# Loading a second layer's weight granules from another engine's queue, one block pair ahead of their split

## The chip, the cores and the metric

One Trainium2 chip, of which the program uses one core. Its engines are named as the profile names them: PE is TensorE's matmuls (PEld its weight loads), DVE is VectorE, ACT is ScalarE, POOL is GpSimd, and SP is SyncE, whose queue issues transfers. The metric is device time in microseconds (us) of one execution, the median of several runs. Less is better.

## The reference, cut to what matters

One inference step of two layers on 4096 prompt rows and 8 sample rows, in float32, width 1024. Layer 0 projects the normalized rows with a 1024 x 3072 matrix, mixes (pooling in four groups, a short convolution, gates), and projects back with a 1024 x 1024 matrix onto the residual. Layer 1 is a windowed attention whose input projection has 2560 columns.

```python
def even_layer(x, ...):          # layer 0
    p = einsum('btd,de->bte', rms_norm(x, g_norm), w_in)
    u, z_a, b_gate, c_gate, v_in, z_b = split(p, EVEN_SPLITS)
    d = pool_mix(u, ...)
    y_a = blockdiag(d, pool_w) * pool_scale * silu(z_a)
    y_b = b_gate * short_conv(c_gate * v_in, ...) * silu(z_b)
    return x + concat(y_a, y_b) @ w_out
# layer 1: q, k, v, z = split(rms_norm(x, g) @ w_in_odd); o = sliding_window_attention(q, k, v)
#          x = x + (o * silu(z)) @ w_out_odd
```

## The kernel before, in words

Every product is made of three passes over a high and a low part of both factors, so each weight is first split: ScalarE writes the high part (a copy to a rounded type), VectorE the difference. `split` (line 80) and `parts` (line 206) do that.

**Layer 0** (lines 176 to 746) runs over six chunks of rows, `L0_CHUNKS`: one of 384, four of 768, one of 640. For each chunk `mixers` goes through 12 pairs of 128-column blocks of the input projection (`pair`, line 444), and `outproj` (line 657) then makes the output projection in two halves of 512 columns. From the second chunk on a pair is a two-by-two product with seven partial products instead of eight, 84 matmuls of 128x384, in an order that is written out in lines 480 to 497: `px`, `py` and `pz` are its three banks of PSUM, and between the products ScalarE copies a bank away (`kept`: first `p1`, then `u2`, then `p5`) before TensorE may add the next product to that bank or VectorE may use it. Each pair first gets its weights by `operands`: four loads on SP's queue, split as they come (tiles `wr`, `wh`, `wl`, three buffers each).

A half of `outproj` is 144 matmuls of 128x512: four quarters `q`, each with one loaded weight tile (`wro`, split to `who` and `wlo`), times six row tiles. Each row tile has a bank (`pso`). When a tile's last quarter is done, VectorE adds the residual (`xr`, loaded by SP in line 668) to it (line 711), SP stores the sum (line 712), and the bank is free for the same row tile of the second half. There are two buffers for `xr`: a third tile's residual is loaded only when the first tile's sum has been stored.

**Layer 1's weights** are prepared during layer 0's chunks 2 to 5: `wq` is a list of 56 granules of 128 x 512. `convert` (line 267), called once a pair and twice in pairs 5 and 11, so 14 times a chunk, does this: it stores the granule of the call before (line 272, SP, 512 KB), loads a new one into a buffer (line 279 or 281, SP, 256 KB), and splits it (ScalarE line 287, VectorE line 288; for the last 16 granules lines 69 and 72). The buffers `cv` have the tag "x", of which there are two, so a load waits for the store of the granule two before it. Layer 1 reads the split granules later.

**Order.** In layer 0 the program text does not fix where an instruction stands in its engine's queue: the framework's scheduler places each as soon as its inputs are expected, and each engine then works through its own queue in that order. The granules of a chunk are therefore not spread over its 12 pairs but stand around the end of the previous chunk's `outproj` and the chunk's first pairs.

Of the kernel before, what the change touches and what calls it, by code (L numbers as in the profile page):

```python
# [9 lines left out]
F32R = mybir.dt.float32r  # L10
U8 = mybir.dt.uint8
AF = mybir.ActivationFunctionType
ALU = mybir.AluOpType
# [4 lines left out]
P = 128  # L18
# [36 lines left out]
def hybrid_kernel(  # L55
# [7 lines left out]
    act, dve, pool, pe, sp = nc.scalar, nc.vector, nc.gpsimd, nc.tensor, nc.sync  # L63

    def f(ap):
        return ap.bitcast(F32)
# [13 lines left out]
    def split(hi, lo, src):  # L80
        acopy(hi, src)
        sub(lo, src, f(hi))
# [15 lines left out]
    gt = cst.tile([P, 2, KT], F32, tag="gt", name="gt")[:, 0]  # L98
# [12 lines left out]
    def granule(key):  # L111

        kind, c, k = key
        if kind == "z":
            e0 = 1536 + c * 256
            return w_in1[:, 2 * k:2 * k + 2, e0:e0 + 256], [2 * k, 2 * k + 1]
        if kind == "in":
            return w_in1[:, k, c:c + 512], [k]
        return w_out1[:, k, c:c + 512], []

    wq = {key: dram.tile([P, 2, 512], F32, tag=f"wq{i}", name=f"wq{i}") for i, key in enumerate(
        z_cols(range(4)) + cols("in", 0) + cols("in", 1024) + cols("in", 512) + cols("out", 0)
        + cols("out", 512))}
# [52 lines left out]
    with ExitStack() as l1:  # L176
# [3 lines left out]
        xp = l1.enter_context(tc.tile_pool(name="xp1", bufs=2))  # L180
# [81 lines left out]


        todo = list(wq)
        converted = []

        def convert(n=1):

            for _ in range(n):
                if converted:  # L270
                    key, t = converted.pop()
                    sp.dma_start(wq[key], f(t))
                if todo:
                    key = todo.pop(0)
                    t = xp.tile([P, 2, 512], F32R, tag="x", name="cv", bufs=2)
                    raw = f(t[:, 1])
                    src, gains = granule(key)
                    if len(gains) > 1:
                        sp.dma_start(raw.rearrange("p (k e) -> p k e", k=2), src)
                    else:  # L280
                        sp.dma_start(raw, src)
                    if not gains:
                        split(t[:, 0], t[:, 1], raw)
                    w = 512 // max(len(gains), 1)
                    for i, kt in enumerate(gains):
                        c = slice(i * w, i * w + w)
                        act.activation(t[:, 0, c], raw[:, c], AF.Copy, scale=gt[:, kt:kt + 1])
                        dve.scalar_tensor_tensor(out=t[:, 1, c], in0=raw[:, c],
                                                 scalar=gt[:, kt:kt + 1], in1=f(t[:, 0, c]),
                                                 op0=ALU.mult, op1=ALU.subtract)  # L290
                    converted.append((key, t))

        def load_out(src):
            raw = wp.tile([P, 2, 512], F32, tag="wr", name="wro", bufs=3)
# [131 lines left out]
        def mixers(ci, X, yh, yl, side=iter(())):  # L426
            t0, n = L0_CHUNKS[ci]
# [5 lines left out]
            w = WX = L + hs  # L433
# [10 lines left out]
            def pair(i, blocks, out11, out12, out22, mid=None):  # L444

                if plain:
                    for e in range(2):
                        wh, wl = block_parts(blocks[e], e == 1)
                        ps = bank("ps")
                        for kt in range(KT):  # L450
                            for k, (u_, v_) in enumerate(((wh, hh), (wh, hl), (wl, hh))):
                                pe.matmul(ps, lhsT=u_[:, kt // 4, kt % 4, :], rhs=v_[:, kt, :],  # L452
                                          start=kt == 0 and k == 0, stop=kt == KT - 1 and k == 2)
                        if e == 0:
                            out11(ps, None)
                            if mid is not None:
                                mid()
                    return ps
                gr = operands(ci, i)
                if ci > 1:  # L460
                    convert(2 if i in (5, 11) else 1)

                def mm(ps, a, b, start=False):


                    gi, at = AT[a]
                    wh, wl = gr[gi]
                    xh, xl, o = B[b]
                    for kt in range(4):
                        for i, (u_, v_) in enumerate(((wh, xh), (wh, xl), (wl, xh))):  # L470
                            pe.matmul(ps, lhsT=u_[:, at, kt, :], rhs=v_[:, o, kt, :],  # L471
                                      start=start and kt == 0 and i == 0, stop=kt == 3 and i == 2,
                                      skip_group_check=True)

                def kept(ps, name):
                    t = tp.tile([P, WX], F32, tag="cp", name=name, bufs=2)[:, :w]
                    acopy(t, ps)
                    return t

                x = bank("px")  # L480
                mm(x, "A11", "B11", start=True)
                p1 = kept(x, "p1")
                y = bank("py")
                mm(y, "A12", "B21", start=True)
                out11(y, p1)
                if mid is not None:
                    mid()
                mm(x, "S2", "T2")
                u2 = kept(x, "u2")
                z = bank("pz")  # L490
                mm(z, "S1", "T1", start=True)
                p5 = kept(z, "p5")
                mm(x, "S3", "T3")
                out22(x, p5)
                mm(z, "S4", "B22")
                out12(z, u2)
                mm(x, "A22", "T4")
                return x

            def plus(out, a, b):  # L500
# [15 lines left out]
            for g in range(4):  # L516
# [76 lines left out]
                for pi in range(NP):  # L593
                    vv, c = vs[pi], cs_[pi]
                    src = c21 if pi == 0 else vv[:, 2:2 + w]
# [5 lines left out]
                    t = tp.tile([P, WX], F32, tag="dl", name="t")  # L601
                    dve.tensor_scalar(out=t[:, :L], in0=vv[:, 0:L], scalar1=cw[:, 0, g:g + 1],
                                      scalar2=None, op0=ALU.mult)
                    for k in (1, 2):
                        dve.scalar_tensor_tensor(out=t[:, :L], in0=vv[:, k:k + L],
                                                 scalar=cw[:, k, g:g + 1], in1=t[:, :L],
                                                 op0=ALU.mult, op1=ALU.add)
# [125 lines left out]
        for ci in range(1, len(L0_CHUNKS)):  # L733
            n = L0_CHUNKS[ci][1]
            last = ci + 1 == len(L0_CHUNKS)
            yh, yl = (yp.tile([P, KT, n + (NS + 40 if last else 0)], F32R, tag=t, name=t)
                      for t in ("yh", "yl"))
            mixers(ci, nxt, yh, yl)
            if not last:
                side = prep(ci + 1)  # L740
                nxt = next(side)
                for _ in side:
                    pass
            if last:
                convert()
            outproj(ci, yh, yl, yh[:, :, n + NS:] if last else None)

    DEBUG = globals().get("DEBUG_L1")
# [11 lines left out]
    xp = ctx.enter_context(tc.tile_pool(name="xp2", bufs=1))  # L760
# [768 lines left out]
```

## Time and profile before

| what | value |
|---|---|
| median of three runs | 3276.95 us (3274.37 to 3279.48) |
| the profiled execution | 3273.23 us |
| its span, first to last instruction | 3271.5 us |
| mean granted TensorE clock | 0.984 of full speed |
| PE busy in the span | 3088.4 us |
| DMA | 541.85 MB, nearly all by SP's queue |

The profile is of one execution; its time is below the lowest of the three runs. A stretch is given in us from the span's start. The granted clock is a share of 2.4 GHz. "Idle before" of an instruction is the time in which its engine had nothing to do, with the instruction or transfer whose end let it go on.

### The profile page before, as it was taken

What the parts mean: (1) busy time and instruction counts of PE and PEld (TensorE: products, weight loads), DVE (VectorE), ACT (ScalarE), POOL (GpSimd) and SP (SyncE); (2) the same over time, 40 slices, a digit from 0 to 9 for tenths busy, and PEclk for the clock granted to TensorE, in tenths of its full rate; (3) what the DMA queues carried; (4) which work ended last, traced back from release to release, by engine and by line L of the source; (5) the groups of instructions that cost most, each with busy time, mean ns of one, the idle gap of its engine ahead of it and who ended that gap; (6) DMA issues with size and microseconds to landing.
All of it is one profiled execution on the core that took longest, in us unless ns stands there. A gap on an engine that the chain in (4) does not pass through costs nothing.

```text
span 3271.5 us, 46047 instructions
## 1 busy us (share of the span) xinstructions
PE 3088.4 (94%) x15926; PEld 2673.6 (82%) x15926; DVE 2148.7 (66%) x4244; ACT 1600.6 (49%) x3701; POOL 870.6 (27%) x1229
## 2 busy tenths in 40 slices
PE   7999999999999999998999999999999999999877
PEld 7888889979979979977778888888878788876665
DVE  5668757767767667831675866758668576685851
ACT  4433434444444444422574655646547466463650
POOL 3244201101111010001332542535325244243420
PEclk9999999999999999999999999999999999999988
DMA  6453375366356357436435546355454553533333
GB/s 186 133 174 127 126 243 172 123 226 206 126 195 229 127 170 262 142 122 222 158 105 187 184 148 216 135 193 184 142 210 142 183 193 136 206 119 123 108 109 134
DMA packets 297922, 541.85 MB, mean 166 GB/s; under 512 B 25272, under 2 KB 159040, under 8 KB 297649
## 3 DMA queue, kind: packets, MB, share of 16 engines
q1 hardware_dynamic: 297689, 538.91, 48.5%
q8 instruction: 126, 2.06, 0.3%
q14 instruction: 107, 0.88, 0.1%
HBM read 462.91 MB, written 78.24 MB: 165 GB/s over the span
## 4 chain that ended last, share of the span: by engine, by line
PE 57%; DVE 16%; DMA 9%; ACT 8%; issue 5%; POOL 5%; SPq 1%; DVEq 0%; POOLq 0%; ACTq 0%
PE px L471 11%; PE pst L838 6%; PE pst L840 6%; PE pst L839 6%; PE pz L471 6%; ACT s L1107 3%; PE ps L452 2%; PE py L471 2%; PE pso L691 2%; PE pso L689 2%; PE pso L693 2%; DMA xr<-x 2%; PE sc L1083 2%; DMA xr<-in_x_prompt_dram 1%; PE psz L927 1%
## 5 line engine op out<-in xcount | busy, mean ns | idle before, releaser
L69 ACT ACTIVATE wh<-wr 128x1024 fp32r<-128x1024 f32 x240 | 227.7, 950 | 231.4 <-PE pz L471 83.4
L211 DVE TENSOR_TENSOR wl<-wr,wh 128x1024 fp32r<-128x1024 f32 x228 | 251.5, 1107 | 104.4 <-ACT wh L69 104.2
L838 PE MATMUL pst<-w,hh 128*128 128x512 f32 x768 | 309.4, 403 | 3.6 <-DVE xr L75 3.5
L840 PE MATMUL pst<-w,hh 128*128 128x512 f32 x768 | 303.5, 395 | 0.0
L839 PE MATMUL pst<-w,hl 128*128 128x512 f32 x768 | 302.7, 394 | 0.0
L1107 ACT ACTIVATE s<-s,st,rq 128x128 f32<-128x128 f32 x512 | 247.2, 484 | 100.1 <-DVE st L1103 99.5
L1127 POOL TENSOR_SCALAR_AFFINE_SELECT qh<-ph 128x512 fp32r<-128x512 f32 x124 | 89.1, 718 | 721.7 <-ACT ph L69 703.7
L471 PE MATMUL px<-th,wh 128*128 128x384 f32 (+1 forms) x720 | 240.4, 334 | 15.0 <-ACT u L69 10.5
L471 PE MATMUL px<-th,wl 128*128 128x384 f32 (+1 forms) x720 | 238.3, 331 | 0.0
L471 PE MATMUL px<-tl,wh 128*128 128x384 f32 (+1 forms) x720 | 238.3, 331 | 0.0
L838 PE MATMUL pst<-w,yh 128*128 128x512 f32 x512 | 209.7, 410 | 8.3 <-DVE xr L75 8.2
L926 PE MATMUL psz<-hh,w 128*128 128x512 f32 x512 | 208.2, 407 | 0.3 <-ACT q L69 0.3
L689 PE MATMUL pso<-who,yh 128*128 128x512 f32 x512 | 201.7, 395 | 6.0 <-DVE xr L75 6.0
L840 PE MATMUL pst<-w,yh 128*128 128x512 f32 x512 | 203.8, 398 | 0.0
L927 PE MATMUL psz<-hl,w 128*128 128x512 f32 x512 | 203.6, 398 | 0.0
L928 PE MATMUL psz<-hh,w 128*128 128x512 f32 x512 | 203.4, 397 | 0.0
L839 PE MATMUL pst<-w,yl 128*128 128x512 f32 x512 | 203.1, 397 | 0.0
L691 PE MATMUL pso<-who,yl 128*128 128x512 f32 x512 | 202.8, 396 | 0.0
L693 PE MATMUL pso<-wlo,yh 128*128 128x512 f32 x512 | 201.6, 394 | 0.0
L838 PEld LDWEIGHTS pst<-w,hh 128*128 128x128 f32 x768 | 145.5, 189 | 31.6 <-DVE xr L75 6.0
L840 PEld LDWEIGHTS pst<-w,hh 128*128 128x128 f32 x768 | 145.1, 189 | 31.6
L839 PEld LDWEIGHTS pst<-w,hl 128*128 128x128 f32 x768 | 145.5, 189 | 25.9
(348 smaller groups left out, 8616.6 us busy)
## 6 DMA issues: line engine op xcount, KB each, us to landing
w<-wq SPq DMA_DIRECT2D x448, 512.0 KB
wr<-in_w_in_even_dram SPq DMA_DIRECT2D x96, 512.0 KB
wr<-wsc SPq DMA_DIRECT2D x96, 512.0 KB
wq<-cv SPq DMA_DIRECT2D x56, 512.0 KB
wro<-in_w_out_even_dram SPq DMA_DIRECT2D x48, 512.0 KB
xr<-in_x_prompt_dram SPq DMA_DIRECT2D x64, 256.0 KB
x<-xr SPq DMA_DIRECT2D x64, 256.0 KB
xt<-x SPq DMA_DIRECT2D x32, 512.0 KB
```

The costliest lines, as they stand in the source:

```text
L69: return act.activation(out, in_, AF.Copy)
L211: (eng or dve).tensor_tensor(out=wl[:, :n], in0=raw, in1=f(wh[:, :n]), op=ALU.subtract)
L471: pe.matmul(ps, lhsT=u_[:, at, kt, :], rhs=v_[:, o, kt, :], start=start and kt == 0 and i == 0, stop=kt == 3 and i == 2, skip_group_check= ...
L689: pe.matmul(acc[i], lhsT=yh[:, kt, ts_], rhs=wh[:, e, :], start=kt == 0, stop=False)
L691: pe.matmul(acc[i], lhsT=yl[:, kt, ts_], rhs=wh[:, e, :], start=False, stop=False)
L693: pe.matmul(acc[i], lhsT=yh[:, kt, ts_], rhs=wl[:, e, :], start=False, stop=kt == KT - 1)
L838: pe.matmul(acc[i], lhsT=xh(kt), rhs=wh, start=kt == 0, stop=False)
L839: pe.matmul(acc[i], lhsT=xl(kt), rhs=wh, start=False, stop=False)
L840: pe.matmul(acc[i], lhsT=xh(kt), rhs=wl, start=False, stop=kt == KT - 1)
L926: pe.matmul(acc[e], lhsT=wh[:, k, es], rhs=xh, start=kt == 0, stop=False)
L927: pe.matmul(acc[e], lhsT=wh[:, k, es], rhs=xl, start=False, stop=False)
L1107: C["exp"] = act.activation(s[:, h, :], s[:, h, :], AF.Exp, bias=nm[:, h:h + 1], scale=r4[:, h:h + 1], accum_out=den[:, h:h + 1])
```

## The change

The three steps of `convert` become three functions. `conv_load` loads a granule, now from ScalarE's queue (`act.dma_start`); `conv_split` splits the granule loaded by the call before; `conv_store` stores it, from SP's queue as before. A pair starts with a split and the next load; in pairs 5 and 11 a store, a split and a load follow in its middle; every pair ends with a store. Buffers, sizes, values and the number of granules stay as they are.

```diff
-        converted = []
-        def convert(n=1):
-            for _ in range(n):
-                if converted:
-                    key, t = converted.pop()
-                    sp.dma_start(wq[key], f(t))
-                if todo:
...
-                    if len(gains) > 1:
-                        sp.dma_start(raw.rearrange("p (k e) -> p k e", k=2), src)
-                    else:
-                        sp.dma_start(raw, src)
...
-                    converted.append((key, t))
+        loaded, parted = [], []
+        def conv_load():
+            if todo:
+                key = todo.pop(0)
+                t = xp.tile([P, 2, 512], F32R, tag="x", name="cv", bufs=2)
+                raw = f(t[:, 1])
+                src, gains = granule(key)
+                act.dma_start(raw.rearrange("p (k e) -> p k e", k=2) if len(gains) > 1 else raw, src)
+                loaded.append((key, t, gains))
+        def conv_split():
+            if loaded:
+                key, t, gains = loaded.pop(0)
...
+                parted.append((key, t))
+        def conv_store():
+            if parted:
+                key, t = parted.pop(0)
+                sp.dma_start(wq[key], f(t))
...
                 gr = operands(ci, i)
                 if ci > 1:
-                    convert(2 if i in (5, 11) else 1)
+                    conv_split()
+                    conv_load()
...
                 if mid is not None:
                     mid()
+                if ci > 1 and i in (5, 11):
+                    conv_store()
+                    conv_split()
+                    conv_load()
                 mm(x, "S2", "T2")
...
                 mm(x, "A22", "T4")
+                if ci > 1:
+                    conv_store()
                 return x
```

What the change does to the queues is shown at three places, all around the end of the first chunk of 768 rows. Lines of the changed kernel have other numbers: its 678 is 668 of before, 722 is 712, 273 and 294 are the load and the store of a granule, 285 the split.

SP's queue, while the first half of `outproj` ends: `xr_3836`, `xr_3840`, `xr_3844`, `xr_3848`, `xr_3852` and `xr_3856` are the residuals of the six row tiles, `x1_3` to `x1_8` the stores of their sums. Before:

```order
L712 DMA x1_3_63<-xr_3836 128x512
L712 DMA x1_4_64<-xr_3840 128x512
L668 DMA xr_3844<-in_x_prompt_dram 128x512
L219 DMA wr_4064<-in_w_in_even_dram 128x8x128
L668 DMA xr_3848<-in_x_prompt_dram 128x512
L246 DMA wr_4070<-wsc0_185 128x1024
L712 DMA x1_5_65<-xr_3844 128x512
L272 DMA wq0_102<-cv_4088 128x1024
L712 DMA x1_6_66<-xr_3848 128x512
L668 DMA xr_3852<-in_x_prompt_dram 128x512
L272 DMA wq1_103<-cv_4241 128x1024
L668 DMA xr_3856<-in_x_prompt_dram 128x512
```

and of the change, after the store of `x1_3`:

```order
L678 DMA xr_3844<-in_x_prompt_dram 128x512
L722 DMA x1_4_64<-xr_3840 128x512
L219 DMA wr_4064<-in_w_in_even_dram 128x8x128
L722 DMA x1_5_65<-xr_3844 128x512
L678 DMA xr_3848<-in_x_prompt_dram 128x512
L294 DMA wq0_102<-cv_4088 128x1024
L678 DMA xr_3852<-in_x_prompt_dram 128x512
L246 DMA wr_4070<-wsc0_185 128x1024
L722 DMA x1_6_66<-xr_3848 128x512
L294 DMA wq1_103<-cv_4240 128x1024
L722 DMA x1_7_67<-xr_3852 128x512
L678 DMA xr_3856<-in_x_prompt_dram 128x512
```

The load of the fourth residual (`xr_3848`) moved from before the third sum's store to behind it, the store of the fourth sum from before to behind the load of the fifth residual, and the load of the sixth from before to behind the store of the fifth sum. The same holds at the ends of the next two chunks; at the fourth, the order of residual loads and stores is the same, with the granules' stores at other places between them.

TensorE's queue in the second half of that `outproj`, whose banks `pso_3860` to `pso_3865` follow those of the first half's six row tiles, at the place where the fifth bank is first used. Before:

```order
L689 MATMUL pso_3863<-who_3910,yh_1662 128x512
L691 MATMUL pso_3863<-who_3910,yl_1663 128x512
L693 MATMUL pso_3863<-wlo_3911,yh_1662 128x512
L689 MATMUL pso_3863<-who_3910,yh_1662 128x512
L689 MATMUL pso_3864<-who_3868,yh_1662 128x512
L691 MATMUL pso_3864<-who_3868,yl_1663 128x512
```

and of the change:

```order
L701 MATMUL pso_3860<-who_3910,yl_1663 128x512
L703 MATMUL pso_3860<-wlo_3911,yh_1662 128x512
L699 MATMUL pso_3861<-who_3910,yh_1662 128x512
L701 MATMUL pso_3861<-who_3910,yl_1663 128x512
L699 MATMUL pso_3864<-who_3868,yh_1662 128x512
L701 MATMUL pso_3864<-who_3868,yl_1663 128x512
```

Counted from the half's first matmul, the fourth bank is first used after 22 matmuls before and after 21 now, the fifth after 46 and now after 32, the sixth after 57 and now after 56. At the ends of the next two chunks the counts are 22, 46, 57 and now 21, 32, 56, at the fourth 23, 48, 60 and now 26, 37, 63.

ScalarE's queue where the next chunk's first pair begins (`p1`, `u2`, `p5` are the copies out of its banks, `cv` the granules). Before, with granules 5 (`cv_4857`), 6 and 7 of the chunk:

```order
L69 ACTIVATE wh_4072<-wr_4070 128x1024
L287 ACTIVATE cv_4857<-cv_4857,gt_100 128x256
L69 ACTIVATE wh_4078<-wr_4076 128x1024
L69 ACTIVATE p1_4107<-px_4094 128x384
L287 ACTIVATE cv_4864<-cv_4864,gt_100 128x256 x2
L287 ACTIVATE cv_5009<-cv_5009,gt_100 128x256
L69 ACTIVATE wh_4084<-wr_4082 128x512
L287 ACTIVATE cv_5009<-cv_5009,gt_100 128x256
L69 ACTIVATE u2_4135<-px_4094 128x384
L69 ACTIVATE dh_4198<-d_4196 128x384
L69 ACTIVATE wh_4218<-wr_4216 128x1024
L69 ACTIVATE p5_4150<-pz_4137 128x384
```

and of the change, with granules 6, 7, 8 (`cv_5169`) and 9 (`cv_5326`):

```order
L285 ACTIVATE cv_4895<-cv_4895,gt_100 128x256 x2
L285 ACTIVATE cv_5008<-cv_5008,gt_100 128x256 x2
L69 ACTIVATE wh_4078<-wr_4076 128x1024
L273 DMA cv_5169<-in_w_in_odd_dram 128x2x256
L69 ACTIVATE p1_4103<-px_4090 128x384
L285 ACTIVATE cv_5169<-cv_5169,gt_100 128x256 x2
L69 ACTIVATE wh_4084<-wr_4082 128x512
L273 DMA cv_5326<-in_w_in_odd_dram 128x2x256
L69 ACTIVATE u2_4131<-px_4090 128x384
L69 ACTIVATE dh_4194<-d_4192 128x384
L285 ACTIVATE cv_5326<-cv_5326,gt_100 128x256 x2
L69 ACTIVATE p5_4146<-pz_4133 128x384
```

Splits of the granules moved forward by about a pair (granule 8 stood ahead of the second pair's `p1` before), and the loads stand in this queue now, granule 8's right ahead of `p1`. At the ends of the next three chunks it is granule 9's load that stands there.

## Rows read from the trace of the kernel before

**Rows 1.** The page, busy time by engine.
```profile
PE 3088.4 (94%) x15926; PEld 2673.6 (82%) x15926; DVE 2148.7 (66%) x4244; ACT 1600.6 (49%) x3701; POOL 870.6 (27%) x1229
```

**Rows 2.** Stretches: us, busy PE PEld DVE ACT POOL (instructions), granted clock, DMA share, GB/s.
```profile
405.00:520.00 115.00, 108.34 (x543) 96.14 (x542) 72.81 (x117) 49.28 (x87) 10.85 (x14) 0.99 0.73 242
...
437.00:440.30 3.30, 3.30 (x10) 2.53 (x9) 1.57 (x3) 0.91 (x2) 0.00 (x0) 0.51 0.76 250
```

**Rows 3.** Waits of PE, 405 to 1310 us: us in total, times, longest.
```profile
PE pso L689 <- DVE xr L75: 6.0, 6, 2.1
PE px L471 <- ACT u L69: 5.8, 6, 1.8
...
PE pz L471 <- ACT p L69: 4.2, 4, 1.4
PE px L471 <- DVE za L75: 2.9, 3, 1.8
PE px L471 <- ACT p L69: 1.3, 1, 1.3
```

**Rows 4.** SP's queue in time, end of the first 768-row chunk: start us, us.
```profile
421.18 0.33 SPq L668 DMA_DIRECT2D xr<-in_x_prompt_dram  x1
...
422.60 0.53 SPq L668 DMA_DIRECT2D xr<-in_x_prompt_dram  x1
...
425.74 0.33 SPq L712 DMA_DIRECT2D x<-xr  x1
...
427.78 0.32 SPq L712 DMA_DIRECT2D x<-xr  x1
431.17 0.33 SPq L668 DMA_DIRECT2D xr<-in_x_prompt_dram  x1
431.55 0.43 SPq L272 DMA_DIRECT2D wq<-cv  x1
433.05 0.33 SPq L668 DMA_DIRECT2D xr<-in_x_prompt_dram  x1
```

**Rows 5.** VectorE in time, the residual adds four to six there.
```profile
427.06 0.69 DVE L75 TENSOR_TENSOR xr<-pso,xr 128x512 f32<-128x512 f32 x1 [0.56 <-DMA xr<-in_x_prompt_dram]
434.95 0.69 DVE L75 TENSOR_TENSOR xr<-pso,xr 128x512 f32<-128x512 f32 x1 [7.19 <-DMA xr<-in_x_prompt_dram]
437.17 0.69 DVE L75 TENSOR_TENSOR xr<-pso,xr 128x512 f32<-128x512 f32 x1 [1.53 <-DMA xr<-in_x_prompt_dram]
```

**Rows 6.** PE in time: second halves of outproj, first and second 768-row chunk.
```profile
432.95 0.39 PE L693 MATMUL pso<-wlo,yh 128*128 128x512 f32 x1
433.18 0.39 PE L689 MATMUL pso<-who,yh 128*128 128x512 f32 x1
435.69 0.50 PE L689 MATMUL pso<-who,yh 128*128 128x512 f32 x1 [2.13 <-DVE xr L75]
...
697.89 0.50 PE L689 MATMUL pso<-who,yh 128*128 128x512 f32 x1 [0.81 <-DVE xr L75]
```

**Rows 7.** The chain of waits, pieces in time: start us, us, what.
```profile
517.01 2.08 PE pz L471 x12
...
744.46 6.58 DMA wq<-cv
...
751.10 2.87 DMA cv<-in_w_in_odd_dram
...
756.51 4.30 DMA wq<-cv
...
760.87 1.81 DMA cv<-in_w_in_odd_dram
```

**Rows 8.** ScalarE in time, first pair of the second 768-row chunk.
```profile
461.97 0.49 ACT L69 ACTIVATE p<-px 128x384 f32<-128x384 f32 x1 [1.27 <-PE px L471]
465.92 0.91 ACT L287 ACTIVATE cv<-cv,gt 128x256 fp32r<-128x256 f32 x2 [3.46 <-DVE xr L75]
```

**Rows 9.** Waits of SP's queue, 405 to 1310 us.
```profile
SPq L281 <- DMA wq<-cv: 26.7, 14, 3.5
```

More of the change, by code (lines that the diff above doesn't have):

```diff
@@ L264, in hybrid_kernel @@
         todo = list(wq)
-        converted = []
-        def convert(n=1):
-            for _ in range(n):
-                if converted:
-                    key, t = converted.pop()
-                    sp.dma_start(wq[key], f(t))
-                if todo:
[L274 to L277, printed above, removed]
-                    if len(gains) > 1:
-                        sp.dma_start(raw.rearrange("p (k e) -> p k e", k=2), src)
-                    else:
-                        sp.dma_start(raw, src)
[L282 to L290, printed above, removed]
-                    converted.append((key, t))
@@ new lines, in hybrid_kernel @@
+        loaded, parted = [], []
[10 more added lines that the diff above has]
+                key, t, gains = loaded.pop(0)
+                raw = f(t[:, 1])
+                if not gains:
+                    split(t[:, 0], t[:, 1], raw)
+                w = 512 // max(len(gains), 1)
+                for i, kt in enumerate(gains):
+                    c = slice(i * w, i * w + w)
+                    act.activation(t[:, 0, c], raw[:, c], AF.Copy, scale=gt[:, kt:kt + 1])
+                    dve.scalar_tensor_tensor(out=t[:, 1, c], in0=raw[:, c],
+                                             scalar=gt[:, kt:kt + 1], in1=f(t[:, 0, c]),
+                                             op0=ALU.mult, op1=ALU.subtract)
+                parted.append((key, t))
@@ L744, in hybrid_kernel @@
             if last:
-                convert()
+                conv_split()
+                conv_store()
             outproj(ci, yh, yl, yh[:, :, n + NS:] if last else None)
```

## The prediction

> **What bounds the kernel now.** I read the busy times first: TensorE is busy for 3088 of 3271.5 us [rows 1], so a change outside it counts only where TensorE waits. I then read the stretches around the ends of the chunks that the change touches. From 405 to 520 us, the end of the first 768-row chunk with the next one's first pairs, TensorE is busy for 108.3 of 115 us [rows 2]: some 7 us are open here, and granules are converted in four such places. TensorE's own waits over all four [rows 3] have two kinds. At the output projection's second half it waits for residual adds, which free the banks: 6.0 us in all. In the first pairs it waits for the copies `u2`, `p5`, `p1` and for a VectorE add behind them: 5.8 + 4.2 + 2.9 + 1.3 = 14.2 us, 3.6 per place. So the most that the conversion can cost now, and the change win, is some 20 us of 3273. I looked at what order SP, TensorE and ScalarE work through at these places, since the scheduler, not the text, decides it.
>
> **The idea does not survive the scheduler.** By its text the change loads with one pair and splits with the next. In ScalarE's queue, though, the loads stand close ahead of splits, and all 14 granules of a chunk within its first two pairs, about one pair earlier than before. What counts is therefore what those orders do.
>
> **Term 1: the residual adds, second half of the output projection.** Here the change moves three transfers on SP's queue: the fourth residual's load goes behind the third sum's store, the fourth sum's store behind the fifth load, the sixth load behind the fifth sum's store. I worked out the first place. TensorE's matmuls follow each other every 0.23 us, and the one at 433.18 is the 46th [rows 6], so the half starts at 433.18 - 45 x 0.23 = 422.8. Before, the fourth load leaves at 422.60 and its add starts at 427.06, the fifth at 431.17 and 434.95, the sixth at 433.05 and 437.17 [rows 4, 5]: 4.46, 3.78 and 4.12 us from issue to add.
> - Fourth: it now leaves behind the store at 425.74, at 426.1; its add starts at 429.9 to 430.5 and ends 0.69 later, at 430.6 to 431.2. TensorE wants that bank after 21 matmuls, at 422.8 + 21 x 0.23 = 427.6: a wait of 3.0 to 3.6 us that was not there.
> - Fifth: its load still waits for the third sum's store (425.74 to 431.17 [rows 4]), so its add still ends at 435.64 and TensorE goes on at 435.69 [rows 5, 6]. It arrives 11 matmuls, 2.5 us, after the fourth's release, at 433.1 to 433.7, and waits 2.0 to 2.6 us. What matters: it has then done 32 matmuls of the half, and had done 46 before.
> - Sixth: after 24 more, at 435.69 + 24 x 0.23 = 441.2. The fourth sum's store now leaves at about 431.9, behind the fifth load and a weight load, and lands 5.27 us later as it did (427.78 to 433.05 [rows 4]), at 437.2; with 4.12 and 0.69 the add ends at 442.0, a wait of 0.8.
>
> Before, the 56 matmuls were done at 435.69 + 10 x 0.23 = 438.0, plus what the clock cost: after the wait of 2.13 us it was granted at 0.51, the lower of the two levels, for 3.3 us [rows 2, 6], which costs 3.3 x 0.49 = 1.6. So 442.0 against 439.6: +2.4 us. If the sixth add is in time it is +1.6, and +4.0 if the clock falls again. At the next two places the fifth add ends the wait as well, and the clock did not fall after a wait of 0.81 [rows 6]: 14 matmuls more behind it are 14 x 0.23 = 3.2 us each; at the last, 48 - 37 = 11 are 2.5. Sum: 2.4 + 3.2 + 3.2 + 2.5 = **11 us**. Bounds: 10.5 (the first at 1.6) and 4.0 + 2 x (3.2 + 0.8 + 1.6) + (2.5 + 0.8 + 1.6) = 20. Nothing covers this, as TensorE is the engine that waits.
>
> **Term 2: ScalarE's copies in the first pairs.** A granule's load waits until the granule two before it is stored. That wait stood on SP's queue (26.7 us in 14 waits for one kind of granule [rows 9]); it now stands in ScalarE's, and what is queued behind it is `p1`, `u2`, `p5` and the split weights, on which TensorE waits. In the first place granule 8's load stands right ahead of `p1` and needs granule 6 stored; granule 6's split stands behind granule 7's load, which needs 5 stored, that needs 3, that needs 1. One cycle of a buffer is a store and a load, 6.58 + 2.87 = 9.45 us at the slow end and 4.30 + 1.81 = 6.11 at the fast one [rows 7], ScalarE's split 0.91 [rows 8], about 0.5 until VectorE's part has followed (my estimate: half of ScalarE's) and an issue of 0.43 [rows 4]: 8.0 to 11.3 us. Granule 1's store leaves at about 432 (431.55 before [rows 4]), so granule 5's leaves two cycles later, at 448 to 454.6, and lands after 4.30 to 6.58, at 452.3 to 461.2. An issue, the split of 6 and its VectorE part take 1.7; but SP holds two residual stores ahead, for sums that exist at about 459 now. So granule 6's store leaves at 459.3 to 463, lands at 463.6 to 469.6, and `p1` is done 0.8 later, at 464.4 to 470.4. `p1` could start at 461.97 [rows 8], and TensorE had 2.08 us of another product to go on with [rows 7]; with 2.4 from term 1 it wants `p1` at 466.5. So it waits 0 to 3.9 us. The five granules after it need half a cycle each, 20 to 28 us, and stand within some 1.6 pairs (a pair is 84 matmuls of 2.08 / 12 us, 14.6), 23 us: another 0 to 5 us, spread over `u2`, `p5` and the next `p1`. In all 0 to 9 us in place of 3.6; between the ends the nearer row is the slow store, as 512 KB beside a DMA share of 0.73 [rows 2] is where these stand, and I take 5.6, so **+2 us a place, +8 us**. Bounds: -14 (all waits of today gone) and 4 x 5.4 = +22.
>
> The Trainium skill ("DMA: Bandwidth & Descriptors", section "Anatomy of one DMA") says that a transfer's semaphore wait is held by the engine that issues it, before dispatch. No row here shows a transfer issued from ScalarE; by that rule the whole wait passes to it, which speaks against the change, and were it otherwise this term would be at its lower bound.
>
> **What costs nothing.** The 56 issues of some 0.33 us each [rows 4] go from SP to ScalarE, 19 us of an engine that is idle for half the span [rows 1]; those ahead of `p1` are in the sum. Splits, bytes and matmuls stay. SP loses 56 issues and their waits, and no wait of TensorE leads to a weight load that was late, so that frees nothing. Layer 1 is untouched: the granules are done earlier, and it starts later by the sum.
>
> **Sum.** 11 + 8 = +19 us on an execution of 3273.2, which is 3.7 below the median; set on the median, 3276.95 + 19 = 3296 us.
>
> **Rivals.**
> - *No change, 3277 us.* TensorE's delay in the second half lets the granules catch up, and the first pairs lose what the second half costs: +11 - 11. For it: both kinds of wait sit in the same 50 us, and term 2 can reach -14. Against it: it needs cycles near 8 us in all four places. The Trainium skill ("DMA: Bandwidth & Descriptors", section "Issuing engines are not separate DMA queues") holds that issuing from several engines only saves issue time; by it nothing would change either, as SP's issue time is not what TensorE waits for.
> - *Faster, 3263 us.* A load leaves ScalarE the moment its buffer is free, no longer behind SP's residual transfers, and the copies are never late: -14. This decides if a buffer's cycle stays under 2 x 23 / 5 = 9.2 us, and the residual transfers, with fewer loads on their queue, free the fifth bank 3.2 us sooner, so that term 1 is nil. Against it: that add hangs on a store and a load which the change leaves alone.
> - *Much slower, 3332 us.* Waits of 2 us and more drop the clock at each place, as at 437 us. Term 1 at its bound, 20, term 2 at its bound, 22, and two more spells of 1.6 a place, 13: +55. For it: two waits over 2 us in a row are forecast. Against it: one such wait is all that the trace shows.
> - *The change does nothing* cannot be: the three queues differ.
>
> **How the numbers follow.** The forecast has a chance of 0.60, no change 0.17, faster 0.10, much slower 0.13. About 0.2% (6.6 us) is what a measurement of this kernel can tell from none. The forecast's own lower end is 10.5 - 14 = -4, a small part of it (0.04) inside that band; its upper end 20 + 22 = +42. The range is 3273 to 3319, which leaves out most of the faster and the much slower case. Faster 0.10; same 0.17 + 0.04 = 0.21; slower 0.69.
>
> **What would show it.** Right: in the second halves TensorE waits for a residual add at the fourth bank for about 3 us and again at the fifth, the waits for adds rising from 6.0 to some 15 us; in the first pairs `p1` starts late, behind a granule's store, and the waits for copies rise from 14 to some 22 us; steady pairs and layer 1 keep their times. Wrong: term 1, if the fifth add ends well before 435; term 2, if granule 6's store lands by 463 or ScalarE does not wait at its loads.

## The result, and the profile after

The changed kernel takes 3310.79 us (median of four runs, 3307.43 to 3317.37), the kernel before beside it 3277.81: a ratio of 1.0106, 95% interval 1.009 to 1.0123. It is slower by 33 us; the forecast was 3296 us, +19, in a range of 3273 to 3319. The profiled execution took 3309.38 us.

The page of the changed kernel, TensorE's busy line [rows 1] and ScalarE's new DMA queue (packets, MB, share of 16 engines):

```profile
PE 3098.8 (94%) x15926; PEld 2683.2 (81%) x15926; DVE 2150.7 (65%) x4244; ACT 1601.7 (48%) x3701; POOL 863.5 (26%) x1229
...
q10 hardware_dynamic: 10112, 14.68, 1.5%
```

The work is the same, 15926 matmuls, yet TensorE is busy for 10 us longer (3098.8 against 3088.4): some of them ran at the lower clock. The four places as stretches (columns as in [rows 2]), each shifted by what the kernel had lost by then, and layer 1. Of the changed kernel:

```profile
405.00:520.00 115.00, 106.40 (x534) 95.32 (x532) 71.59 (x114) 47.81 (x84) 9.05 (x14) 0.97 0.74 242
670.00:785.00 115.00, 103.25 (x513) 92.67 (x512) 67.70 (x99) 43.28 (x67) 8.14 (x14) 0.97 0.73 238
934.00:1069.00 135.00, 120.80 (x600) 109.03 (x599) 79.80 (x116) 52.84 (x81) 10.67 (x16) 0.96 0.68 218
1219.00:1364.00 145.00, 133.67 (x776) 123.01 (x775) 92.56 (x191) 59.00 (x112) 7.29 (x21) 0.98 0.70 225
...
1560.00:3300.00 1740.00, 1641.55 (x8088) 1333.21 (x8088) 1138.35 (x2704) 943.41 (x2628) 612.18 (x862) 0.98 0.47 158
```

and of the kernel before, besides the first place [rows 2]:

```profile
670.00:785.00 115.00, 109.83 (x567) 99.12 (x566) 73.67 (x108) 47.68 (x74) 10.93 (x15) 1.00 0.73 245
925.00:1060.00 135.00, 130.98 (x686) 119.95 (x685) 88.57 (x131) 58.65 (x90) 12.03 (x19) 1.00 0.70 230
1195.00:1340.00 145.00, 139.31 (x834) 129.50 (x833) 100.09 (x211) 64.02 (x123) 9.41 (x23) 1.00 0.71 236
...
1527.00:3267.00 1740.00, 1644.75 (x8098) 1335.78 (x8096) 1140.09 (x2706) 943.72 (x2629) 612.50 (x862) 0.98 0.45 159
```

TensorE's idle time is length less busy time: 6.7, 5.2, 4.0 and 5.7 us before, 8.6, 11.8, 14.2 and 11.3 now, 24 us more in all. The clock falls from 0.99 to 0.97, then from 1.00 to 0.97, 0.96 and 0.98: of 115, 115, 135 and 145 us that is 14 us (the shares are rounded to 0.01, which alone allows 5 either way). Together 38, or 34 with the 10 us that the page's busy times give for the clock, against the 33 by which layer 0's last matmuls start later (1461.6 us before, 1494.7 now). In layer 1 the two stretches of 1740 us, 33 us apart, have busy times 3 us apart. So the loss is made at the four places, some two thirds by waiting and the rest by the clock that falls after the waits.

TensorE's waits, 405 to 1345 us of the changed kernel (us in total, times, longest), against [rows 3]:

```profile
PE px L475 <- ACT u L69: 12.8, 4, 4.1
PE pz L475 <- ACT p L69: 10.5, 7, 3.3
PE px L475 <- ACT p L69: 9.8, 3, 5.9
PE pso L699 <- DVE xr L75: 8.8, 7, 2.1
...
PE px L475 <- DVE za L75: 1.7, 2, 1.4
```

Waits for copies and the add behind them rose from 14.2 to 34.8 us, those for residual adds only from 6.0 to 8.8.

What the copies wait for, ScalarE in time at the first place, where `u2` is the copy `u<-px`, and at the third (ACTq rows are issues of loads):

```profile
459.14 0.38 ACTq L273 DMA_DIRECT2D cv<-in_w_in_odd_dram  x1
459.56 0.49 ACT L69 ACTIVATE p<-px 128x384 f32<-128x384 f32 x1 [2.82 <-DMA wq<-cv]
466.85 0.51 ACT L285 ACTIVATE cv<-cv,gt 128x256 fp32r<-128x256 f32 x1 [6.79 <-DMA cv<-in_w_in_odd_dram]
...
468.18 0.47 ACT L69 ACTIVATE u<-px 128x384 f32<-128x384 f32 x1
...
998.23 0.72 ACT L285 ACTIVATE cv<-cv,gt 128x512 fp32r<-128x512 f32 x1 [7.95 <-DMA cv<-in_w_in_odd_dram]
...
999.81 0.47 ACT L69 ACTIVATE p<-px 128x384 f32<-128x384 f32 x1
```

and TensorE behind them, in time:

```profile
468.70 0.69 PE L475 MATMUL px<-th,wh 128*128 128x384 f32 x1 [4.14 <-ACT u L69]
469.19 0.52 PE L475 MATMUL px<-tl,wh 128*128 128x384 f32 x1
...
1000.33 0.69 PE L475 MATMUL px<-th,wh 128*128 128x384 f32 x1 [5.93 <-ACT p L69]
```

ScalarE stands still for 6.79 and 7.95 us, not at a load that waits for a store, but at a **split** that waits for its load, with the copy behind it. After the wait the matmuls take 0.52 us, where they take 0.33 once the clock is up again (from 733.12 us on, say, in this trace). ScalarE's own waits, 405 to 1345 us, tell how much is of which kind:

```profile
ACT cv L285 <- DMA cv<-in_w_in_odd_dram: 118.0, 31, 12.3
...
ACT cv L69 <- DMA cv<-in_w_out_odd_dram: 43.3, 13, 6.0
```

and before, 405 to 1310 us:

```profile
ACT cv L287 <- DMA cv<-in_w_in_odd_dram: 80.5, 20, 14.0
...
ACT cv L69 <- DMA cv<-in_w_out_odd_dram: 26.2, 8, 10.0
```

Splits waiting for loads: 106.7 us before, 161.3 now. The profile puts another 17 us of the splits' waits before down to the store of a sum and to a residual add, which a split does not read, so the rise is between 38 and 55 us. Waits for stores at a load's place, which I had forecast as the cause, come to 6.5 us of ScalarE's idle time in three waits (2.8 of it ahead of the `p1` shown).

### The profile page after: what moved, and what is told of

The parts are those of the page before. It is cut to its first block, busy times and chain, and to the rows that moved or that the text cites. A ratio compares the mean times of both kernels' runs of the same rounds, so it can differ in the third digit from the quotient of the medians.

```text
span 3307.7 us, 46071 instructions
## 1 busy us (share of the span) xinstructions
PE 3098.8 (94%) x15926; PEld 2683.2 (81%) x15926; DVE 2150.7 (65%) x4244; ACT 1601.7 (48%) x3701; POOL 863.5 (26%) x1229
## 4 chain that ended last, share of the span: by engine, by line
PE 56%; DVE 14%; DMA 12%; ACT 8%; issue 4%; POOL 4%; SPq 1%; ACTq 0%; DVEq 0%; POOLq 0%
PE px L475 11%; PE pst L849 6%; PE pst L851 6%; PE pst L850 6%; PE pz L475 6%; ACT s L1118 3%; DMA cv<-in_w_in_odd_dram 3%; DMA wq<-cv 3%; PE py L475 2%; PE ps L455 2%; DMA xr<-x 2%; PE sc L1094 2%; PE psz L938 1%; PE psz L937 1%; PE psz L939 1%
```

## The experiments

Four things changed together: the queue that loads, the lag of the split, the later store, and the order that the scheduler made of them. The order can be counted. Of each kernel, the granules that stand fully split in ScalarE's queue ahead of the first pair's `p1` at the four places, and the time as a ratio to the kernel before, run beside it:

| kernel | loads from | split ahead of `p1` | median, us | ratio (95%) |
|---|---|---|---|---|
| before | SP | 6, 6, 6, 8 | | 1 |
| changed | ScalarE | 8, 9, 9, 9 | 3310.8 | 1.0106 (1.009 to 1.0123) |
| e1 | SP | 7, 7, 7, 8 | 3278.6 | 1.0015 (1.0003 to 1.0028) |
| e2 | ScalarE | 8, 9, 9, 9 | 3307.7 | 1.01 (1.0072 to 1.0127) |
| e3 | GpSimd | 7, 8, 8, 9 | 3313.3 | 1.0118 (1.0096 to 1.014) |
| e5 | SP | 8, 8, 8, 8 | 3317.7 | 1.014 (1.012 to 1.016) |
| e6 | ScalarE | 6, 6, 6, 6 | 3294.6 | 1.0066 (1.0045 to 1.0086) |
| e9 | GpSimd | 6, 6, 6, 6 | 3306.2 | 1.0106 (1.0086 to 1.0126) |
| e12 | SP | 6, 6, 6, 6 | 3275.4 | 1.001 (0.9994 to 1.0026) |
| e4, paced | ScalarE | 1, 1, 1, 1 | 3263.3 | 0.9973 (0.9958 to 0.9988) |
| e7, paced | SP | 1, 1, 1, 1 | 3261.6 | 0.9972 (0.9959 to 0.9986) |
| e8, paced | SP | 1, 1, 1, 1 | 3262.8 | 0.9972 (0.996 to 0.9984) |
| e10, even | SP | 0, 0, 0, 0 | 3258.9 | 0.9954 (0.9937 to 0.997) |
| e11, first nine | SP | 0, 0, 0, 0 | 3258.5 | 0.9953 (0.9935 to 0.9972) |

The theory at the start: the loads' waits for stores, in ScalarE's queue, hold the copies. Its rivals: the lag and the later store cost; or the splits, which the scheduler moved ahead of the copies, cost.

### Which part of the change: e1 and e2

e1 puts SP's queue back into the changed kernel; e2 makes ScalarE's queue the only edit of the kernel before.

```diff
 # e1, conv_load of the changed kernel
-                act.dma_start(raw.rearrange("p (k e) -> p k e", k=2) if len(gains) > 1 else raw, src)
+                sp.dma_start(raw.rearrange("p (k e) -> p k e", k=2) if len(gains) > 1 else raw, src)
 # e2, convert of the kernel before
-                        sp.dma_start(raw.rearrange("p (k e) -> p k e", k=2), src)
+                        act.dma_start(raw.rearrange("p (k e) -> p k e", k=2), src)
-                        sp.dma_start(raw, src)
+                        act.dma_start(raw, src)
```

> The changed kernel with one word put back: the granules are loaded from SP's queue again; the three-step split (load with one pair, split and store with the next) stays. My theory: what costs is that the load, with its wait for an older granule's store, stands in ScalarE's queue ahead of the copies TensorE wants. Then this is level with the kernel before, 3278 us (3272 to 3284), with TensorE's waits for copies of the first pairs at 12 to 18 us over the four places. Rival: the lag and the later store cost, whichever queue loads; then it stays near 3311 us, with 30 us or more of such waits.

> The kernel before with one edit: the granules' loads are issued from ScalarE's queue; one call still stores, loads and splits. My theory: the queue is the whole of the change, so this is level with the changed kernel, 3311 us (3304 to 3318), with 30 us or more of waits for copies. Rival (lag and late store): 3278 us. If both parts carry a share, it lies between, 3285 to 3303 us.

1.0015 and 1.01: the queue is the whole of it as far as these runs can tell, and the lag and the later store are worth at most 0.28%. The word also sets the order: e2's count of splits ahead of `p1` is the changed kernel's, e1's nearly that of before. So the queue itself and the order are still two candidates.

### The queue or the place of the splits: e3, e5, e6, e9, e12

e3 loads from GpSimd's queue: early splits, but no load in ScalarE's queue.

```diff
-                act.dma_start(raw.rearrange("p (k e) -> p k e", k=2) if len(gains) > 1 else raw, src)
+                pool.dma_start(raw.rearrange("p (k e) -> p k e", k=2) if len(gains) > 1 else raw, src)
```

> The changed kernel with the loads issued from GpSimd's queue: the splits stand in ScalarE's queue as early as in the changed kernel and as close ahead of the copies, but no load and no wait for a store stands there. My theory in its narrow form (the loads' own waits in ScalarE's queue): near 3278 us (3272 to 3288). Rival: the splits cost, since each waits in ScalarE's queue for a load that comes a buffer's cycle later, and their early place in the order is what the change brought; then 3300 to 3320 us, and ScalarE's waits for granule loads at 150 us or more (161 in the changed kernel, 107 before, from the first output projection's end to the last place).

It came out at 1.0118, which I first read as the splits' place alone. e9, below, took that reading back.

e5 leaves the kernel before as it is, loads on SP's queue, and holds the copies behind as many granules as the changed kernel has ahead of them (`tc.add_manual_dep` orders the scheduler only, and adds no wait of an engine for a semaphore):

```diff
+        PULLED = {7: (0, "p1"), 8: (0, "u2"), 9: (0, "p5"), 11: (1, "p1"), 12: (1, "u2")}
...
+                    at = PULLED.get(k % 14)
+                    c_ = copies.get((k // 14 + 2, *at)) if at else None
...
+                    if c_ is not None:
+                        tc.add_manual_dep(c_.ins, hi.ins.name, NOSYNC, reason="behind the split")
```

> The kernel before (loads from SP's queue, one-step granules) with one thing of the changed kernel: an order for the scheduler alone that puts the copies p1, u2, p5 of each place behind as many granule splits on ScalarE as the changed kernel has ahead of them (eight ahead of the first p1, where there were six). Theory of the position: the copies are late because more splits stand ahead of them, and each split holds ScalarE until its load, a buffer's cycle later, has come; then 3298 us (3290 to 3312) with 28 us or more of waits for copies over the four places, though no load stands in ScalarE's queue. Theory of the queue (the load's own wait for a store in ScalarE's queue): 3278 us (3272 to 3284), waits as before (14 us).

1.014, more than the changed kernel and above the range that I had given (3290 to 3312). ScalarE in time at the first place of e5:

```profile
467.05 0.91 ACT L294 ACTIVATE cv<-cv,gt 128x256 fp32r<-128x256 f32 x2 [6.04 <-DVE xr L75]
...
471.08 0.47 ACT L69 ACTIVATE p<-px 128x384 f32<-128x384 f32 x1
```

`p1` stands behind two granules more and starts at 471.08, 9.1 us later than before [rows 8]. **Splits forced ahead of the copies can cost as much as the whole change, without any load in ScalarE's queue.** But they do not cost it by the same waits alone. TensorE waits for `u2` and `p1` for 20.6 us in e5 (7.1 before, 22.6 in the changed kernel), and for nearly as long where neither of the two kernels waits at all, at splits of weights (`wh`) and of the mixing's `d` (`dh`):

```profile
PE px L480 <- ACT wh L69: 8.9, 8, 2.1
PE psd L587 <- ACT dh L69: 8.0, 4, 2.6
```

So e5 shows what the place can cost, not that it makes up the changed kernel's loss. That it is above the changed kernel is left open; it also holds the second pair's copies.

e6 is the mirror: the changed kernel with the later splits held behind the copies where they stood before. e9 and e12 differ from it in the loading queue alone.

```diff
+        BEHIND = {6: (0, "p1"), 7: (0, "p1"), 8: (0, "p5"), 9: (1, "p1"), 10: (1, "p1"),
+                  11: (1, "u2"), 12: (1, "p5"), 13: (2, "p1")}
...
+                def behind(i):
+                    if c_ is not None:
+                        tc.add_manual_dep(i.ins, c_.ins.name, NOSYNC, reason="not ahead of the copy")
 # e9
-                act.dma_start(...
+                pool.dma_start(...
 # e12
-                act.dma_start(...
+                sp.dma_start(...
```

> The changed kernel (loads from ScalarE's queue) with the splits of the seventh and later granules of each place held behind the copies that they stood behind before the change, again by an order for the scheduler alone. Theory of the position: the waits for copies fall back to 12 to 20 us and the time to 3282 us (3274 to 3292), though every load still stands in ScalarE's queue. Theory of the queue: the loads still wait for stores ahead of the copies, 3300 to 3315 us.

> The late splits of the run before last group (seventh and later granules of a place behind the copies they stood behind before the change), with the loads issued from GpSimd's queue in place of ScalarE's. With ScalarE's queue and late splits 11 to 13 us of the change's 33 were given back and some 22 stayed. If these 22 are the loads' own waits for stores in ScalarE's queue, they go: 3278 us (3272 to 3286), waits for copies 14 to 18 us. If the position of the splits still holds them, or something else of the change (the granules start earlier, in the output projection), it stays at 3290 to 3300 us.

> The late splits once more, with the loads from SP's queue: against the same splits with loads from ScalarE's (3295 us) and from GpSimd's queue (3306 us) only the queue that holds the loads differs. If what the late splits left of the change's cost (some 22 us) is the loads' wait for stores inside a queue that TensorE's copies or their inputs also pass, then on SP's queue, which carries neither, it goes: 3276 us (3269 to 3283), waits for copies 10 to 18 us, at the level of the kernel before. If the rest is due to the three-step split or to the forced order itself, it stays at 3288 us or more.

Half and half: e6 gives back 0.40% of the changed kernel's 1.06% and keeps 0.66%, between the two ranges that I had given, where SP's queue (e12) has 0.1%. So with the same forced order the queue still costs some 0.56% or 18 us (0.3 to 0.8 by the intervals). In e6 loads hold ScalarE's queue up, as the semaphore waits of line 275 show, which loads the granules (count, ns minimum, median, maximum, first and last start):

```profile
L275 ACTq EVENT_SEMAPHORE  x53: 17/17/5662, 429.6 to 1290.1; - x53
```

The Trainium skill ("DMA: Bandwidth & Descriptors", section "Anatomy of one DMA") has a transfer's semaphore wait happen on the issuing sequencer, before dispatch; e6's row agrees. ScalarE's idle time that a granule's store ended is 11.9 us in e6, 6.5 in the changed kernel and none in e12. But most of it stands ahead of weight splits and not of copies:

```profile
ACT wh L69 <- DMA wq<-cv: 9.4, 3, 4.4
```

And the forced order does not fix everything. Ahead of the second pair's `u2` stand 10, 11, 11 and 10 granules in e6 and 10, 10, 10 and 9 in e12, and TensorE's longest wait at e6's four places is of the old kind, behind a split whose load is still out. ScalarE:

```profile
752.46 0.72 ACT L297 ACTIVATE cv<-cv,gt 128x512 fp32r<-128x512 f32 x1 [5.58 <-DMA cv<-in_w_in_odd_dram]
...
753.91 0.47 ACT L69 ACTIVATE u<-px 128x384 f32<-128x384 f32 x1
```

and TensorE:

```profile
754.43 0.69 PE L487 MATMUL px<-th,wh 128*128 128x384 f32 x1 [4.37 <-ACT u L69]
```

So the queue has a cost beyond the granules ahead of the first `p1`, but how its 18 us divide between loads that wait in ScalarE's queue and splits that still stand elsewhere is open.

e9, which was to free ScalarE of these waits, came out at 3306 us, above both of its ranges and no better than e3 within the noise. GpSimd's waits in e9, 405 to 1345 us:

```profile
POOL cv L275 <- DMA wq<-cv: 148.5, 27, 14.7
```

That engine makes other copies for the chunk (its `u`, `ucar` and `vcar` of the mixing), which share the queue with such waits. That these are what TensorE then lacks was not tried, so where GpSimd's queue costs is open, and e3 tells nothing on the splits' place.

### Without the bunching: e4, e7, e8

The scheduler puts 14 granules around two pairs. In these kernels a granule's load may not stand ahead of the last matmul traced, that of the pair before: in e4 with ScalarE's loads, in e7 with SP's, in e8 in the kernel before.

```diff
+                    last_mm[:] = [pe.matmul(ps, ...)]
...
+                if last_mm:
+                    tc.add_manual_dep(ld.ins, last_mm[0].ins.name, NOSYNC, reason="not ahead of the pair before")
```

> The changed kernel, loads from ScalarE's queue as there, with an order added for the scheduler alone: a granule's load stands behind the last matmul of the pair before, so that one granule (two in pairs 5 and 11) falls into each pair and the bunches at the chunk ends are gone. My theory: a load in ScalarE's queue costs only where the older granule is not yet stored; with a pair of 14.6 us per granule it always is. Then the waits for copies fall to 0 to 5 us in all, those for residual adds to 6 us or less, and the time to 3262 us (3255 to 3272). Rival: an issue and a split more in every one of 48 pairs holds some copy each time by about 0.4 us, 48 x 0.4 = 19 us: 3280 to 3300 us.

> The paced kernel (one granule a pair) with the loads from SP's queue in place of ScalarE's, the three-step split kept. Theory of the position: once no split stands ahead of a copy with its load still out, the queue that loads does not matter: 3263 us (3257 to 3270), waits for copies 0 to 6 us. Rival: on SP's queue a paced load stands behind the pair's weight loads and residual transfers and comes later than its split's place, so ScalarE waits at splits again in each pair: 3270 us or more.

> The kernel before with the same pacing and nothing else of the change. Theory of the position: the bunching was the cost in both kernels, and the three-step split adds nothing to the pacing: 3263 us (3257 to 3270), 10 to 20 us under the kernel before. Rival: without the lag a paced split stands right behind its load and ScalarE waits for it for about a load (2 to 4 us) in each pair; where a copy stands behind it, that costs 0.5 us in some of 48 pairs, 3270 to 3285 us.

All three agree, 0.9973, 0.9972 and 0.9972. A queue that costs 0.56% with bunched granules costs nothing that these runs can tell (0.2%) when each has a pair for itself, and the lag brings nothing here either. ScalarE's waits at the granules' splits in e4:

```profile
ACT cv L69 <- DMA cv<-in_w_out_odd_dram: 2.4, 2, 2.1
...
ACT cv L287 <- DMA cv<-in_w_in_odd_dram: 0.8, 2, 0.7
```

3.2 us, where the changed kernel has 161. What was left is TensorE's wait for the next chunk's rows:

```profile
PE tr L415 <- DVE xt L341: 11.6, 15, 2.7
```

### A version that beats both: e10 and e11

Rows and granules share the two "x" buffers, and the paced granules hold them up to the last pair. e10, on SP's queue and paced like e7, loads behind the pair's first product, splits behind `u2` and stores at the pair's end, with none in the last pair; e11 is done after nine pairs, `[1, 2, 2, 2, 2, 2, 1, 1, 1, 0, 0, 0]`.

```diff
+                n = [1, 1, 2, 1, 1, 2, 1, 1, 2, 1, 1, 0][i] if ci > 1 else 0
                 x = bank("px")
                 mm(x, "A11", "B11", start=True)
+                for _ in range(n):
+                    conv_load()
...
                 u2 = kept(x, "u2")
+                for _ in range(n):
+                    conv_split()
...
+                for _ in range(n):
+                    conv_store()
                 return x
```

> A version meant to beat both: one granule a pair, loaded from SP's queue behind the pair's first product, split behind u2 and stored at the pair's end, two in pairs 2, 5 and 8, none in the last pair, so that no granule holds one of the two shared x buffers when the next chunk's rows are loaded. In the paced kernels TensorE waited 10 to 14 us for the normalized rows of the next chunk (5 before). If the held x buffer is the reason, these fall to 5 us or less and the time to 3254 us (3248 to 3261), 0.5% under the kernel before; rival: the rows are late for another reason, and it is level with the paced kernels, 3262 us (3257 to 3268).

> The same with the granules in the first nine pairs, two each in pairs 1 to 5, so that three pairs are left free ahead of the next chunk's rows. If rows are late because granules hold the x buffers in the last pairs, this is the best of the paced kernels, 3250 us (3244 to 3258), with waits for normalized rows at 5 us or less; if two granules a pair bring back splits that wait for their loads ahead of the copies, waits for copies rise to 8 us or more and it is 3262 us or slower.

0.9954 and 0.9953, 15 us under the kernel before and some 50 under the changed one; the two cannot be told apart, and both medians lie at the upper edge of what was expected or just above it. The waits of e10, 405 to 1345 us:

```profile
PE tr L415 <- DVE xt L341: 5.5, 10, 1.1
PE px L475 <- DVE za L75: 5.3, 5, 1.6
PE pz L475 <- ACT p L69: 1.9, 5, 0.6
PE pso L699 <- DVE xr L75: 1.7, 4, 0.8
PE px L475 <- ACT u L69: 0.9, 2, 0.7
```

The waits for rows are back at 5.5 us, as expected if the held buffer was the reason (e10 moved the loads and splits within the pair as well, so this is not shown apart); copies and the add behind them cost 8.1 us where it was 14.2, residual adds 1.7 where it was 6.0. The first of its places as a stretch:

```profile
405.00:520.00 115.00, 113.55 (x588) 102.82 (x587) 71.88 (x109) 46.16 (x75) 8.93 (x15) 1.00 0.56 183
```

The DMA share is 0.56 there, not 0.73, and the clock stays at 1.00.

## Why the prediction was right or wrong

**The time: inside the range, in part by luck.** +33 us against the forecast of +19: term 1 was 8 too high, the copies and the clock together 23 to 27 too low, and the errors cancel in part.

**The sign and the place: right.** The loss lies in the first pairs at the four places; layer 1 is unchanged. "The idea does not survive the scheduler" holds: e1 and e2 show that the order it makes follows from the queue.

**Term 1, the residual adds, 11 us: wrong; it was 2.8.** The step that failed is "it now leaves behind the store at 425.74, at 426.1": I moved the fourth load behind the third sum's store, but left that store at its old time. SP in time, changed kernel:

```profile
422.76 0.33 SPq L722 DMA_DIRECT2D x<-xr  x1
423.18 0.38 SPq L678 DMA_DIRECT2D xr<-in_x_prompt_dram  x1
...
426.02 0.33 SPq L678 DMA_DIRECT2D xr<-in_x_prompt_dram  x1
```

The third sum's store is off at 422.76, 3.0 us earlier, and the fourth and the fifth load behind it are earlier too. It starts with the first sum. VectorE's first add, before:

```profile
418.45 0.68 DVE L75 TENSOR_TENSOR xr<-pso,xr 128x512 f32<-128x512 f32 x1
```

and of the changed kernel:

```profile
414.44 0.69 DVE L75 TENSOR_TENSOR xr<-pso,xr 128x512 f32<-128x512 f32 x1
```

The first sum's store leaves right behind this add, at 419.16 before and at 415.16 now, and with it the third residual's load. The add is 4.0 us earlier: VectorE's steps for the next chunk's rows run 1.8 us earlier, and four of them no longer stand ahead of it. The granules' loads, which are gone from SP's queue here, did not hold that store: the last was issued by 416.12. Why the scheduler moved the add is not shown. VectorE's fifth add, changed kernel:

```profile
429.24 0.69 DVE L75 TENSOR_TENSOR xr<-pso,xr 128x512 f32<-128x512 f32 x1 [1.60 <-DMA xr<-in_x_prompt_dram]
```

At 429.24, 5.7 us ahead of the old [rows 5]: the sign that I had named against the term ("well before 435"). TensorE waits 1.71 us once, at the fourth bank, and not at the fifth. The relief that I had put into the rival "faster", and argued away since "that add hangs on a store and a load which the change leaves alone", took place; the store itself came earlier.

**Term 2, ScalarE's copies, from 14.2 to 22 us: right in kind, too small.** They came to 34.8, +21 in place of +8. Three steps failed.
- *One place stood for four.* I worked out the first, with eight granules ahead of `p1`, and multiplied by four; the other three have nine. The idle times grew by 1.9 us at the first place (I had +2), and by 6.6, 10.2 and 5.6 at the others. That the first agrees is luck: the wait that I had worked out there did not come, and another did.
- *What holds the copy.* I had `p1` behind a load that waits for granule 6's store ("granule 6's store leaves at 459.3 to 463"). It left at 453.93 and had landed by 459.14, and `p1` ran at 459.56, 2.4 us earlier than before: the sign that I had named against it. SP's two residual stores ahead of it, which I had put at about 459 with term 1's delay, left at 452.37, so term 1's error went into term 2. The wait was one step on, `u2` behind the split of granule 8, in the chain of waits of the changed kernel:

```profile
453.93 5.13 DMA wq<-cv
...
459.14 7.68 DMA cv<-in_w_in_odd_dram
```

- *The price of a load.* I took 1.81 to 2.87 us from [rows 7]; here it is 7.68, and 7.12 at the third place. The chain of the kernel before could have told. It has this load, 9 us ahead of those in [rows 7], and, right behind their piece of 1.81 us, this copy:

```profile
735.34 5.14 DMA cv<-in_w_in_odd_dram
...
762.69 0.38 ACT u L69
```

The piece of 1.81 us ends where the chain goes over to `u2`, which reads no granule, so it is not a load's time.

The cycle of a buffer, the number on which the term rests, was right as the cause; its load was priced at less than half. The changed kernel against e6 shows what the early splits cost (0.40%), e6 against e12 what the queue costs besides (0.56%, some of it still at splits).

**The clock, 14 us: left out of the sum.** It stood in the rival "much slower" alone, as "two more spells of 1.6 a place, 13". The size was right, 10 us by the busy times and 14 by the shares; but the clock fell behind the waits, most of them term 2's, so it should have stood in the sum with them. The sum in the forecast's own terms is then 2.8 + 21 + 10 to 14, or 34 to 38, of which 33 are seen at the end of layer 0.

**"What costs nothing".** The 56 issues on ScalarE were rightly put at nothing: e4 and e7 differ in the queue alone and by 0.01%, where 0.2% could be told. For paced granules the Trainium skill's rule ("DMA: Bandwidth & Descriptors", section "Issuing engines are not separate DMA queues"), by which several issuing engines only save issue time, agrees with that pair of runs. For bunched ones the measurement differs from it and decides: e2, with nothing but another issuing engine, is 1% slower. What stands behind the transfer in the issuer's queue, and the order that the scheduler makes of it, counted here.

## What to carry to other kernels

Where a scheduler makes the order, choosing the queue of a transfer is choosing an order too: look at what the scheduler then puts ahead of the instructions that the bound engine waits for, place by place, and not at the first place alone. Look for two things on an engine that others wait for: a transfer that waits in its queue, and a consumer that stands there with its transfer still out. Here most of the changed kernel's waits for copies were of the second kind. Background work with few buffers is best given a steady pace, one piece for each unit of the main work: in this kernel neither the queue nor the lag mattered then, and it gained 0.3 to 0.5%.

## What the runs showed of the hardware

- The time of a granule's load, 256 KB each, varied by a factor of two and a half and more. In e9 it was, over all 56 (minimum, median, maximum):

```profile
DMA to landing us min/median/max: 2.8/4.2/7.4
```

  In the changed kernel the one at 459.14 took 7.68, where the DMA share over the place is 0.74.
- After waits of 3.31 to 5.93 us the clock was at its lower level for some microseconds (0.50 from 1000.33 to 1004 us, behind the longest). The stretch behind the wait of 3.39 us at 728.84, changed kernel:

```profile
728.00:736.00 8.00, 7.16 (x32) 7.16 (x33) 5.47 (x9) 2.85 (x6) 0.40 (x2) 0.79 0.92 278
```

A mean of 0.79 of full speed over 8 us, between the two levels (0.5 and 1): by my estimate 8 x 0.21 = 1.7 us lost, half of the wait itself. At the four places it was 0.96 to 0.98 in the changed kernel and 1.00 in the paced ones.
